# Attention on one core: scores for 1024 queries at a time with 512 moving columns, weight sums per query pair, and the first V loads held

## The chip, the cores and the metric

The kernel runs on one core of a Trainium2 chip. The metric is the device time of the whole program in microseconds (us). PE is TensorE, PEld its weight loads, DVE is VectorE, ACT ScalarE, POOL GpSimd, SP SyncE.

## The reference

```python
# q, k, v: (8, 2048, 512) float32
scores = np.matmul(q, k.transpose(0, 2, 1)) / np.sqrt(512)
attn_weights = special.softmax(scores, axis=-1)
return np.matmul(attn_weights, v)
```

## The kernel before

Both matrix products are done as blocks of two by two with seven products in place of eight: the operands' sums are made on DVE, the products' sums on ACT and DVE, or in the bank (the stretch of accumulator memory) that the matmuls add up in. A batch is 4 blocks of 512 queries (one block is a "quarter" below). While PE multiplies the weights of block g with V (the PV products), it also scores block g+1 (the QK products), in 28 "slots" that alternate the two kinds. Only the first block's scores are done plainly, with eight products, since nothing has been summed yet.

The QK product of a group (cut): two pairs of key blocks, 256 queries each, so four matmuls of 256 columns.

```python
for j in range(G):              # G = 2 pairs of key blocks, QH = 256 queries
    for c in range(2):
        nc.tensor.matmul(
            dst[:, j * QH:(j + 1) * QH], lhs[:, j, c, :], rhs[:, :, c, :],
            start=(n in (1, 5) and j == 0 and c == 0), stop=(c == 1), ...)
```

The weight sums for PV are made for a whole group as soon as its last exponential is there, for all 256 columns (cut):

```python
def p_sums(g, n):
    js = slice(n * G, (n + 1) * G)
    a11, a21 = left[0][:, js], right[:, js, 0]
    a12, a22 = left[1][:, js], right[:, js, 1]
    return [lambda: add(s1[:, js], a21, a22), lambda: sub(s2[:, js], s1[:, js], a11),
            lambda: sub(a21, a11, a21), lambda: sub(s4[:, js], a12, s2[:, js])]
```

At the start Q's and K's first chunks are transposed on PE, later ones by DMA. The first four V loads are issued ahead of the loads of Q's third and fourth chunks (cut):

```python
load("k", 0, 1, (2, 2)); load("k", 0, 2); load("k", 0, 3, ...); load("q", 0, 1, ...)
for c in range(NCH):
    load_v(0, c)
load("q", 0, 2, ...); load("q", 0, 3, ...)      # these two are transposed by DMA
```

The softmax here doesn't subtract the row's maximum and nothing guards it: scores larger than these inputs give would overflow.

Of the kernel before, what the change touches and what calls it, by code (L numbers as in the profile page):

```python
# [12 lines left out]
def kernel(  # L13
# [26 lines left out]
    EXP = mybir.ActivationFunctionType.Exp  # L40
    MULT = mybir.AluOpType.mult
# [4 lines left out]
    QTW = 512  # L46
    NQS = QTW // P
    NQT = T // QTW
# [4 lines left out]
    QH = QTW // 2  # L53
    VP = D + 8
    TP = H + 8
    inv_sqrt_d = float(1.0 / np.sqrt(D))

    G = 2
    NG = NJ // G
    COPY = mybir.ActivationFunctionType.Copy  # L60

    const = ctx.enter_context(tc.tile_pool(name="const", bufs=1))
    stage = ctx.enter_context(tc.tile_pool(name="stage", bufs=4))
    kpool = ctx.enter_context(tc.tile_pool(name="kpool", bufs=5))
    qpool = ctx.enter_context(tc.tile_pool(name="qpool", bufs=3))
    vpool = ctx.enter_context(tc.tile_pool(name="vpool", bufs=2))
    ppool = ctx.enter_context(tc.tile_pool(name="ppool", bufs=2))
    opool = ctx.enter_context(tc.tile_pool(name="opool", bufs=4))
# [18 lines left out]
    qT, kT = {}, {}  # L87
    staged = {}
    vs = {}
# [33 lines left out]
    def operands(what):  # L123
        pool = kpool if what == "k" else qpool
        raw = pool.tile([P, CH, ND, P], F16, tag=what + "raw")
        sums = [pool.tile([P, 2, 2, P], F16, tag=what + f"s{n}", name=what + f"s{n}") for n in (1, 2, 4)]
        return [raw] + sums

    def dma_transpose(what, b, c):
        src = staged.pop((what, b, c))  # L130
        t = operands(what)
        nc.sync.dma_start_transpose(
            out=t[0][:].rearrange("p n c r -> p (n c) r"),
            in_=src[:].rearrange("p n d -> p (n d)"),
        )
        (kT if what == "k" else qT)[b, c] = t

    def transposed(what, b, c, n, src, w, copy):
        if n == 0:
            (kT if what == "k" else qT)[b, c] = operands(what)  # L140
        t = (kT if what == "k" else qT)[b, c]
        tr = psum["px"].tile([P, 2, ND, P], F16, tag="px", name="tr")
        for m in range(w):
            for dc in range(ND):
                nc.tensor.transpose(  # L145
                    tr[:, m, dc, :], src[:, n + m, dc * P:(dc + 1) * P], ident[:]
                )
        copy(out=t[0][:, n:n + w], in_=tr[:, 0:w])

    def pe_transpose(what, b, c, n0=0, n1=CH):  # L150
        src = staged[what, b, c]
        for n in range(n0, n1, 2):
            transposed(what, b, c, n, src, 2, nc.scalar.copy if n else nc.vector.tensor_copy)
        if n1 == CH:
            staged.pop((what, b, c))

    def first_transpose(what, n):
        transposed(what, 0, 0, n, staged[what, 0, 0], 1, nc.vector.tensor_copy)

    def k_blocks(t):  # L160
        w = t[0][:].rearrange("p (j s) c r -> p j s c r", s=2)
        return w[:, :, 0, 0:2], w[:, :, 0, 2:4], w[:, :, 1, 0:2], w[:, :, 1, 2:4]

    def q_blocks(t):
        w = t[0]
        return w[:, 0:2, 0:2], w[:, 2:4, 0:2], w[:, 0:2, 2:4], w[:, 2:4, 2:4]
# [3 lines left out]
    def k_sums(b, c):  # L170
        t = kT[b, c]
        a11, a12, a21, a22 = k_blocks(t)
        _, s1, s2, s4 = t
# [7 lines left out]
    def q_sums(b, c):  # L181
        t = qT[b, c]
        b11, b12, b21, b22 = q_blocks(t)
        _, t1, t2, t4 = t
        return [
            lambda: sub(t1[:], b12, b11),
            lambda: sub(b12, b22, b12),  # L187
            lambda: sub(t2[:], b22, t1[:]),
            lambda: sub(t4[:], b21, t2[:]),
        ]  # L190

    def new_v(b):
        vh = vpool.tile([P, NJ, 2, VP], F16, tag="vh")
        t1 = vpool.tile([P, NJ, TP], F16, tag="t1")
        t2 = vpool.tile([P, NJ, H], F16, tag="t2")
        t4 = vpool.tile([P, NJ, H], F16, tag="t4")
        nc.gpsimd.memset(vh[:, :, 1, D:D + 1], 1.0)
        nc.gpsimd.memset(t1[:, :, H:H + 1], 1.0)
        vs[b] = (vh, t1, t2, t4)

    def load_v(b, c):
        dst = vs[b][0][:].rearrange("p j s d -> p (j s) d")
# [3 lines left out]
    def v_sums(b, c):  # L206
        vh, t1, t2, t4 = vs[b]
# [4 lines left out]
            lambda: sub(t1[:, js, 0:H], b12, b11),  # L212
            lambda: sub(b12, b22, b12),
            lambda: sub(t2[:, js], b22, t1[:, js, 0:H]),
            lambda: sub(t4[:, js], b21, t2[:, js]),  # L215
        ]

    def new_p(g):
        left = [ppool.tile([P, NJ, QH], F16, tag=f"left{s}", name=f"left{s}") for s in range(2)]
        right = ppool.tile([P, NJ, 2, QH], F16, tag="right")  # L220
        sums = [ppool.tile([P, NJ, QH], F16, tag=f"s{n}", name=f"s{n}") for n in (1, 2, 4)]
        pts[g] = (left, right, sums)
# [4 lines left out]
    def plain_tile(g, kb):  # L227

        b, qt = divmod(g, NQT)
        if kb == 0:  # L230
            new_p(g)
        st = bank("qz" if kb % 3 == 2 else "qx")
        c, n = divmod(kb, CH)
        for dc in range(ND):
            nc.tensor.matmul(  # L235
                st[:], kT[b, c][0][:, n, dc, :], qT[b, qt][0][:, :, dc, :],
                start=(dc == 0), stop=(dc == ND - 1),
            )
        left, right, _ = pts[g]
        exp(left[kb % 2][:, kb // 2, :], st[:, 0:QH])  # L240
        exp(right[:, kb // 2, kb % 2, :], st[:, QH:QTW])

    def plain_half(g, j, half):

        b, qt = divmod(g, NQT)
        if j == 0 and half == 0:
            new_p(g)
        st = bank("qx")
        kt, qt_ = kT[b, j // G][0], qT[b, qt][0]
        for s in range(2):  # L250
            for dc in range(ND):
                nc.tensor.matmul(
                    st[:, s * QH:(s + 1) * QH], kt[:, 2 * (j % G) + s, dc, :],
                    qt_[:, 2 * half:2 * half + 2, dc, :],
                    start=(s == 0 and dc == 0), stop=(dc == ND - 1), skip_group_check=True,
                )
        left, right, _ = pts[g]
        if half:
            exp(right[:, j], st[:].rearrange("p (s q) -> p s q", s=2))
        else:  # L260
            for s in range(2):
                exp(left[s][:, j, :], st[:, s * QH:(s + 1) * QH])

    class Group:


        def __init__(self, g, n):
            self.g, self.n = g, n
            self.js = slice(n * G, (n + 1) * G)
            b, qt = divmod(g, NQT)  # L270
            self.a, self.b = kT[b, n], qT[b, qt]

        def product(self, n):
            a11, a12, a21, a22 = k_blocks(self.a)
            b11, b12, b21, b22 = q_blocks(self.b)
            _, s1, s2, s4 = self.a
            _, t1, t2, t4 = self.b
            if n == 1:
                if self.n == 0:
                    new_p(self.g)  # L280
                self.left, self.right, _ = pts[self.g]
# [13 lines left out]
            for j in range(G):  # L295
                for c in range(2):
                    nc.tensor.matmul(  # L297
                        dst[:, j * QH:(j + 1) * QH], lhs[:, j, c, :], rhs[:, :, c, :],
                        start=(n in (1, 5) and j == 0 and c == 0), stop=(c == 1),
                        skip_group_check=True,  # L300
                    )
            getattr(self, f"after{n}", lambda: None)()

        def two(self, t):
            return t[:].rearrange("p (j q) -> p j q", j=G)

# [5 lines left out]
        def after5(self):  # L312
            self.cz = czpool.tile([P, G, 2, QH], F32, tag="cz")
            nc.scalar.copy(out=self.cz[:, :, 1, :], in_=self.two(self.z))  # L314

        def after6(self):
            nc.scalar.copy(out=self.cz[:, :, 0, :], in_=self.two(self.x))  # L317

        def after7(self):
            nc.vector.tensor_add(self.cz[:, :, 1, :], self.two(self.x), self.cz[:, :, 1, :])  # L320

        def after3(self):
            nc.vector.tensor_add(self.cz[:, :, 0, :], self.two(self.z), self.cz[:, :, 0, :])  # L323

        def after4(self):
            exp(self.left[1][:, self.js, :], self.two(self.x))

        def after2(self):
            exp(self.left[0][:, self.js, :], self.two(self.y))

        def exp_right(self):
            exp(self.right[:, self.js], self.cz[:])

    def p_sums(g, n):
        left, right, (s1, s2, s4) = pts[g]
        js = slice(n * G, (n + 1) * G)
        a11, a21 = left[0][:, js], right[:, js, 0]
        a12, a22 = left[1][:, js], right[:, js, 1]
# [6 lines left out]

    class Pair:
# [3 lines left out]
        def __init__(self, g, i):  # L350
            self.g, self.i, self.done = g, i, 0

        def product(self, n):
            g, i = self.g, self.i
            left, right, (s1, s2, s4) = pts[g]
            vh, t1, t2, t4 = vs[g // NQT]
            cols = slice(i * P, (i + 1) * P)
            self.apart = g == NP - 1 and i == 1
            own = "q" if self.apart else "p"
# [4 lines left out]
            elif n == 5:  # L364
# [4 lines left out]
                3: (lambda j: s4[:, j, cols], lambda j: vh[:, j, 1, H:D + 1], "z"),  # L369
                4: (lambda j: right[:, j, 1, cols], lambda j: t4[:, j, :], "x"),  # L370
                5: (lambda j: s1[:, j, cols], lambda j: t1[:, j, 0:H + 1], "z"),
                6: (lambda j: s2[:, j, cols], lambda j: t2[:, j, :], "x"),
# [22 lines left out]
        def store(self, o, half, ds=slice(0, D)):  # L395
            b, qt = divmod(self.g, NQT)
# [273 lines left out]
```

## Time and profile before

| | before |
|---|---|
| device time, median of 3 | 807.06 us |
| span of the profiled run | 805.1 us |
| PE busy, weight loads busy | 99%, 88% |
| DVE busy, ACT busy | 73%, 71% |
| matmuls | 7244 |

The lines themselves stand in the prediction. The reading that counts for PE is from start to start: what one matmul adds to the time.

### The profile page before, as it was taken

The numbers are of one execution on the slowest core, as the hardware profiler recorded it, in microseconds if no ns is written. First come the engines' busy times: TensorE is split into PE (matmuls) and PEld (weight loads), VectorE is DVE, ScalarE is ACT, GpSimd is POOL, SyncE is SP. The second block draws the span as 40 slices with busy tenths as digits, with TensorE's granted clock in tenths as the row PEclk, the third lists the DMA queues.
The fourth block names the chain that finished last, engine by engine and source line by source line (L and its number), as shares of the span: only waits on it lengthen the run. The fifth ranks groups of instructions, "written<-read, shape, count | busy, mean of one in ns | idle before, by whom it ended". The sixth has DMA issues, their size and how long they took to land.

```text
span 805.1 us, 18445 instructions
## 1 busy us (share of the span) xinstructions
PE 798.2 (99%) x7244; PEld 705.1 (88%) x7244; DVE 591.4 (73%) x1477; ACT 571.1 (71%) x1039; POOL 72.7 (9%) x117
## 2 busy tenths in 40 slices
PE   8999999999999999999999999999999999999998
PEld 5788888888888888888888888888888888888887
DVE  4977787787767778677777777777777777766653
ACT  5767767767767777677677677677777776776773
POOL 4020103000030000300002000110002001000000
PEclk9999999999999999999999999999999999999999
DMA  9999966989379992998829997299972998921112
GB/s 207 202 182 179 166 129 116 209 151 183 92 125 216 153 173 70 155 219 142 154 79 162 208 152 154 64 183 197 172 142 67 189 198 158 156 69 46 54 40 79
DMA packets 190246, 116.56 MB, mean 145 GB/s; under 512 B 124496, under 2 KB 172880, under 8 KB 190160
## 3 DMA queue, kind: packets, MB, share of 16 engines
q0 software_dynamic: 49648, 49.29, 39.5%
q1 hardware_dynamic: 140368, 66.08, 39.3%
q8 instruction: 56, 0.92, 0.5%
q14 instruction: 30, 0.25, 0.1%
q10 hardware_dynamic: 144, 0.03, 0.0%
HBM read 100.70 MB, written 33.55 MB: 167 GB/s over the span
## 4 chain that ended last, share of the span: by engine, by line
PE 96%; DVE 2%; DMA 2%; POOL 0%; ACT 0%; issue 0%; SPq 0%; DVEq 0%
PE t L380 48%; PE t L297 46%; DMA stage<-in_k_dram 1%; PE t L235 1%; DMA first<-in_q_dram 1%; PE tr L145 0%; POOL stage L107 0%; DVE t L215 0%; DVE o L391 0%; DVE cz L323 0%; DVE right L342 0%; DVE s L340 0%; ACT o L388 0%; DVE raw L187 0%; DVE s L341 0%
## 5 line engine op out<-in xcount | busy, mean ns | idle before, releaser
L297 PEld LDWEIGHTS <-raw 128*128 128x128 f16 x1984 | 194.1, 98 | 23.4 <-issue 0.6
L388 ACT ACTIVATE o<-t,r 128x256 f32<-128x256 f32 x256 | 122.5, 478 | 128.6 <-DVE r L408 105.7
L297 PE MATMUL t<-raw 128*128 128x256 f16 x1488 | 203.0, 273 | 0.0
L225 ACT ACTIVATE left<-t 128x512 f16<-128x512 f32 (+1 forms) x264 | 156.8, 595 | 21.4 <-PE t L297 18.9
L380 PEld LDWEIGHTS <-s 128*128 128x128 f16 x1536 | 150.3, 98 | 18.5 <-issue 0.2
L297 PEld LDWEIGHTS <-ks 128*128 128x128 f16 x1488 | 145.6, 98 | 17.9 <-issue 0.8
L391 DVE SCALAR_TENSOR_TENSOR o<-t,r,o 128x256 f32<-128x256 f32 x192 | 92.4, 482 | 81.3 <-PE t L380 48.3
L297 PE MATMUL t<-qs,ks 128*128 128x256 f16 x992 | 139.0, 273 | 0.5 <-ACT t L310 0.4
L225 ACT ACTIVATE right<-cz 128x1024 f16<-128x1024 f32 x124 | 132.7, 1070 | 1.5 <-DVE cz L320 1.5
L380 PE MATMUL t<-t,s 128*128 128x257 f16 (+1 forms) x1024 | 133.1, 273 | 0.0
L380 PE MATMUL t<-vh,left 128*128 128x256 f16 x1024 | 132.7, 273 | 0.0
L314 ACT COPY cz<-t 128x512 f32<-128x512 f32 x124 | 72.8, 587 | 67.3 <-PE t L297 67.3
L380 PEld LDWEIGHTS <-right 128*128 128x128 f16 x1024 | 100.2, 98 | 12.2 <-issue 0.6
L320 DVE TENSOR_TENSOR cz<-t,cz 128x512 f32<-128x512 f32 x124 | 85.2, 687 | 34.6 <-PE t L297 34.6
L380 PEld LDWEIGHTS <-left 128*128 128x128 f16 x1024 | 100.2, 98 | 11.6
L323 DVE TENSOR_TENSOR cz<-t,cz 128x512 f32<-128x512 f32 x124 | 84.8, 684 | 1.9 <-PE t L297 1.9
L297 PE MATMUL t<-qs,raw 128*128 128x256 f16 x496 | 74.4, 273 | 0.5 <-DVE cz L320 0.5
L297 PE MATMUL t<-raw,ks 128*128 128x256 f16 x496 | 74.4, 273 | 0.0
L340 DVE TENSOR_TENSOR s<-right 128x512 f16<-128x512 f16 x128 | 54.0, 422 | 27.2 <-ACT right L225 22.2
L317 ACT COPY cz<-t 128x512 f32<-128x512 f32 x124 | 73.2, 591 | 0.2 <-PE t L297 0.2
L310 ACT COPY t<-t 128x512 f32<-128x512 f32 x124 | 70.7, 570 | 3.3 <-ACT o L388 0.3
L380 PE MATMUL t<-vh,s 128*128 128x257 f16 x512 | 66.7, 273 | 0.0
(51 smaller groups left out, 614.1 us busy)
## 6 DMA issues: line engine op xcount, KB each, us to landing
out_dram<-o SPq DMA_DIRECT2D x127, 256.0 KB, 2.8
vh<-in_v_dram POOLq DMA_DIRECT2D x32, 512.0 KB, 14.9
stage<-in_k_dram POOLq DMA_DIRECT2D x29, 512.0 KB, 8.5
stage<-in_q_dram POOLq DMA_DIRECT2D x28, 512.0 KB, 10.3
vh<-in_q_dram POOLq DMA_DIRECT2D x3, 512.0 KB, 20.3
raw<-stage SPq DMA_TRANSPOSE x56, 6.5
first<-in_q_dram SPq DMA_DIRECT2D x2, 256.0 KB, 3.6
first<-in_k_dram SPq DMA_DIRECT2D x2, 256.0 KB, 3.8
```

The source lines that it names most:

```text
L225: nc.scalar.activation(out=out_, in_=in_, func=EXP, scale=inv_sqrt_d)
L235: nc.tensor.matmul(st[:], kT[b, c][0][:, n, dc, :], qT[b, qt][0][:, :, dc, :], start=(dc == 0), stop=(dc == ND - 1),)
L297: nc.tensor.matmul(dst[:, j * QH:(j + 1) * QH], lhs[:, j, c, :], rhs[:, :, c, :], start=(n in (1, 5) and j == 0 and c == 0), stop=(c == 1) ...
L310: nc.scalar.copy(out=self.y[:], in_=self.x[:])
L314: nc.scalar.copy(out=self.cz[:, :, 1, :], in_=self.two(self.z))
L317: nc.scalar.copy(out=self.cz[:, :, 0, :], in_=self.two(self.x))
L320: nc.vector.tensor_add(self.cz[:, :, 1, :], self.two(self.x), self.cz[:, :, 1, :])
L323: nc.vector.tensor_add(self.cz[:, :, 0, :], self.two(self.z), self.cz[:, :, 0, :])
L340: lambda: add(s1[:, js], a21, a22),
L380: nc.tensor.matmul(dst[:, 0:width], lhs(j), rhs(j), start=(first and j == 0), stop=(j == NJ - 1), skip_group_check=True,)
L388: nc.scalar.activation(out=out_, in_=src, func=COPY, scale=r[:])
L391: nc.vector.scalar_tensor_tensor(out=out_, in0=src, scalar=r[:], in1=out_, op0=MULT, op1=ADD)
```

## The change

The intent is fewer, longer instructions for the same arithmetic. 1024 queries are scored together, so that a product of one pair of key blocks has 512 moving columns (columns of the operand that streams past the loaded weights). PV is unchanged in shape. To make room, weight sums are held for one pair of query blocks (128 columns each) at a time instead of for the whole block, K's operands and V's sums are single-buffered, and V's sums fall into one quarter. The plainly scored first part is now 1024 queries. The core of the diff, with cuts:

```diff
-    QTW = 512
+    QH = 512
+    QW = 2 * QH
...
-            for j in range(G):
-                for c in range(2):
-                    nc.tensor.matmul(
-                        dst[:, j * QH:(j + 1) * QH], lhs[:, j, c, :], rhs[:, :, c, :],
...
+            for dc in range(2):
+                nc.tensor.matmul(
+                    dst[:], lhs[:, j, dc, :], rhs[:, :, dc, :],
+                    start=(n in (1, 5) and dc == 0), stop=(dc == 1),
...
+    def p_sums(g, which, j0=0, j1=NJ):
...
+                spool.tile([P, NJ, P], F16, tag=f"s{n}", name=f"s{n}") for n in (1, 2, 4)
...
+    FIRST = "a1 a5 b1 a3 a2 a6 a7 b5 a4 b3 b2 b6".split()
...
+        return {2 * n + (5 if g == 0 else 1): x for n, x in enumerate(order)}
...
+    VSUMS = (0, 1, 2, 3, 5, 6, 8, 10, 12, 14, 15, 16, 17, 18, 19, 20)
...
+    dma_transpose("q", 0, 2)
+    dma_transpose("q", 0, 3)
+
+    nc.gpsimd.tensor_copy(out=gate[:], in_=qraw[1][:, 2 * NT - 1, ND - 1, 0:1])
+    for c in range(NCH):
+        load_v(0, c)
```

The copy into `gate` reads the last element that the second of the two transposes writes. The V loads stand behind it in GpSimd's program: in the trace the copy waits 18.67 us for that transpose, which lands at 31.90, and the first V load is issued at 32.48. This is "the hold".

## The prediction

> **What bounds the kernel now.** I read the page's busy line first, then the chain of waits, then the tensor engine's timeline, because only start-to-start distances tell a busy tensor engine from one at its peak.
>
> ```profile
> PE 798.2 (99%) x7244; PEld 705.1 (88%) x7244; DVE 591.4 (73%) x1477; ACT 571.1 (71%) x1039; POOL 72.7 (9%) x117
> ...
> PE 96%; DVE 2%; DMA 2%; POOL 0%; ACT 0%; issue 0%; SPq 0%; DVEq 0%
> ```
>
> PE is busy 99% of the span and carries 96% of the chain that ended last; VectorE and ScalarE have a quarter of the span free. Now the PE timeline in mid-kernel (start, length, line, operation, shapes, count):
>
> ```profile
> 303.36 0.60 PE L297 MATMUL t<-raw 128*128 128x256 f16 x4
> 303.79 0.60 PE L297 MATMUL t<-qs,ks 128*128 128x256 f16 x4
> 304.23 1.04 PE L380 MATMUL t<-vh,s 128*128 128x257 f16 x8
> 305.11 0.60 PE L297 MATMUL t<-qs,ks 128*128 128x256 f16 x4
> 305.55 0.60 PE L297 MATMUL t<-qs,raw 128*128 128x256 f16 x4
> 305.98 0.27 PE L380 MATMUL t<-vh,left 128*128 128x256 f16 x1
> ```
>
> Take start to start, not the printed lengths, which overlap. 303.36 to 305.98 holds 24 matmuls: 2.62/24 = 109.2 ns each, with no gap. L297 is the scores (QK), L380 weights times V (PV). And the same view at the start, where the kernel already has matmuls of 512 columns:
>
> ```profile
> 16.48 1.07 PE L145 MATMUL tr<-ident,stage 128*128 128x128 f16 x16 [0.33 <-DMA stage<-in_k_dram]
> 17.38 3.62 PE L235 MATMUL t<-raw 128*128 128x512 f16 x16
> 20.84 1.06 PE L145 MATMUL tr<-ident,vh 128*128 128x128 f16 x16
> ...
> 27.80 0.60 PE L297 MATMUL t<-raw 128*128 128x256 f16 x4
> ```
>
> Sixteen of 512 columns take 20.84 - 17.38 = 3.46 us, 216.2 ns each. Two of 256 take 218.4. The seven-product stream starts at 27.80. Last, the PE waits after 30 us, and windows of one quarter of a batch each:
>
> ```profile
> PE t L297 <- DVE cz L320: 0.5, 1, 0.5
> ```
>
> ```profile
> 297.00:321.50 24.50, 24.50 (x227) 21.96 (x225) 19.93 (x50) 17.73 (x33) 0.00 (x0) 1.00 0.39 99
> 321.50:346.00 24.50, 24.50 (x227) 21.91 (x225) 17.09 (x42) 17.73 (x33) 6.10 (x10) 1.00 0.94 153
> ```
>
> The columns are length, PE, PEld, DVE, ACT, POOL busy, granted clock, DMA share, GB/s. PE never idles in them even where DVE is at 19.9 of 24.5. One listed wait of 0.5 us in 775: there is no wait here for a change to remove.
>
> **What the Trainium skill says.** (1) "TensorE: Matmul & The Clock Gate", section "Wait — 56ns, not 53.3ns?": a warm matmul starts N/2.4 GHz plus about 2.5 ns after the one before. That gives 109.2 ns at 256 and 215.8 at 512; the trace agrees (109.2, 216.2). So halving the instruction count at equal columns saves about 2.5 ns per pair and no more. (2) The same page, "Back-to-back issue gap", has about 131 ns for each N=512 matmul in a stream with weight loads. The trace shows 216.2 in just such a stream, so I do not use it; on it, one would hope for 140 us. (3) "Perfetto Trace Analysis", section "Identifying the Most-Contended Engine", prefers LDWEIGHTS busy to matmul busy as the measure of headroom. It is 88% here, and the change cuts it; but the distance between matmuls is that of columns alone, so fewer weight loads should buy nothing. (4) "VectorE: DVE Perf Modes", section "Side-by-side: where the cycles go for N=2048 bf16": some 150 cycles fixed, plus half a cycle per element for a two-tensor 16-bit op. For 512 elements 414 cycles, 431 ns; the trace has 417 to 425. For 1024 I estimate 0.69 us (0.42 + 256 cycles at 0.96 GHz).
>
> **The change part by part.**
>
> Scores, main stream. Before: 31 blocks of 512 queries x 4 groups x 7 products x 4 matmuls = 3472, of 256 columns: 3472 x 109.2 = 379.1 us. After: 15 spans of 1024 queries x 8 groups x 7 x 2 = 1680, of 512 columns: 1680 x 215.9 = 362.7. That is **-16.4 us**, but 12.1 of it is that one block of 512 queries leaves the stream; the instruction saving alone is 4.3.
>
> Scores of the first span, in plain form. Before 12 key blocks x 4 matmuls of 512 columns, and 32 of 256. After, 28 tiles x 4 of 512 and the same 32 of 256: 64 more at 216 ns = **+13.8 us**. The 12.1 us of seven products come back as 13.8 of eight, on the path, as PE alone sets the end. The sum of PE work is **-2.6 us**.
>
> PV: 32 x 2 x 7 x 8 = 3584 matmuls before and after, same shapes. Nothing.
>
> Weight sums: 128 x 4 ops of 512 elements become 64 x 4 of 1024 (some split): 512 x 0.42 = 215 us against 256 x 0.69 = 177. Q's sums fall likewise. DVE has about 40 us less work, all beside PE: worth nothing directly, but it pays for denser places. V's 16 sums now fall into one quarter of a batch instead of two. Counted from start to start (some 0.05 us below the printed lengths, as neighbours overlap) that quarter has: 8 cz additions 5.0, 6 final additions 2.6, 4 reciprocals 0.5, pair sums 5.1 plus 0.5 for the split, V sums 5.9, one of Q 0.6: some 20 of 24.3 us. That is the 19.9 at which no PE gap shows above. ScalarE's work per group is unchanged, 17.7 of 24.5.
>
> Start. The plain part runs after the same first 9.3 us of loads. The first Q and K chunks land when they did; the second Q chunk takes the landing slot of K's third chunk (16.43), just in time for its transposes at 16.5; K's third and fourth slip to about 19.5 and 22, and are wanted after some 23 us and 31 us. So the stream starts at 27.80 + 13.8 = 41.6. Q's other two chunks land near 24.5 and 27 (2.5 us apart, as the V loads before: 24.38, 26.90, 29.41 in the list of DMA issues), their transposes at 4.5 us more, near 31.6. Only then V's loads are issued: the first about 6 us later (a lone 512 KB load took 5.7 to 6.7), the others 2.5 apart: 38, 40.5, 43, 45.5. The first PV product stands at slot 5 of the stream, near 43.8, its last two key blocks want the fourth load: PE waits **about 1 us** there. DVE, which is strictly in order, stands at V's sums meanwhile and then has about 18 us of work in 19: I give that **0.7 us**.
>
> End. Without scores now run two quarters instead of one: 112 more PV products with nothing between. Before, the last 128 took 786.76 to 801.5, 14.7 us for 14.0: 0.7 lost. I add **0.5 us** for the second, and **0.5 us** in all for the dense batch starts and single-buffered K, whose transposes have at least 14 slots of 0.87 us to land, for a median of 6.5.
>
> Against this about 1.5 us of small gaps near 27.8 to 48 go and are re-made; I count half of it gone: -0.8. Sum: -2.6 + 1.0 + 0.7 + 0.5 + 0.5 - 0.8 = **-0.7 us**, rounded toward the careful tuning that the held V loads betray: -1.3. Predicted **805.8 us**.
>
> **The rivals.** (a) Pure PE arithmetic: all new waits are hidden. For it: DVE and ACT slack, and no PE waits before. Then -2.6 to -4, 803 to 804.5. (b) The start becomes DMA-bound: the V loads, held behind two transposes, come several us late. For it: DMA is at nine tenths in the first slices, and a transpose that shared it took 10 us against 4.5. Against: after the two Q chunks nothing else is queued. It costs 3 to 5 us once: 808 to 811. (c) Single-buffered K and V sums, and the crowded DVE, stall every batch. Against: each overwrite stands behind its last reader by one slot or more. At 1 us per batch, 7 us: 812; for slower by 2% it would need over 2 us per batch, 16 in all. (d) 512-column matmuls or half as many weight loads free PE far more, as the 131 ns or the 88% would suggest. Against: 216 ns measured. Then tens of us, below 780.
>
> **Range and chances.** (a) and my sum together carry most; (b) is the likeliest miss, (c) the tail. Range 802.8 to 811. Two per cent is 16 us: faster needs (d), 0.01; slower needs (c) at its worst, 0.03; within, 0.96.
>
> **What would show it.** Right: L297's main group of about 1680 matmuls at 216 ns start to start; PEld busy well down (by some 170 us) with no gain from it; the stream's first product near 41.6; V's last load landing near 45 with a PE wait of 1 us; DVE busy some 40 us less. Wrong: main-stream distances other than 216; PE gaps repeated every 98 us by a DVE or DMA releaser; a start later than 43; or a wait of several us in the last 25.

## The result, and the profile after

The changed kernel took 806.44 us (median of 4, 805.94 to 807.17) against 806.98 for the kernel before (median of 4). The ratio is 0.9993, with a 95% interval of 0.9976 to 1.0011: no difference is shown. A ratio here is the mean time of one kernel's fast runs over that of the other's of the same rounds, so it is not quite the ratio of the medians.

The page's busy line and chain of the changed kernel:

```profile
PE 796.4 (99%) x5516; PEld 536.1 (67%) x5516; DVE 548.5 (68%) x1213; ACT 570.8 (71%) x1021; POOL 71.4 (9%) x104
...
PE 91%; DMA 6%; SPq 1%; POOL 1%; DVE 0%; issue 0%; ACT 0%; ACTq 0%; POOLq 0%
```

1728 matmuls and as many weight loads are gone. Weight-load time fell by 169 us and DVE by 43 us, yet the span is the same, 805.4 against 805.1 us. New is the 6% of DMA in the chain, where 2% stood.

The PE timeline in mid-kernel (start, length, engine, line, operation, shapes, count); L278 is now QK, L373 PV:

```profile
303.37 1.04 PE L373 MATMUL t<-vt,right 128*128 128x256 f16 x8
304.24 0.59 PE L278 MATMUL t<-qraw,kraw 128*128 128x512 f16 x2
304.67 0.59 PE L278 MATMUL t<-qs,ks 128*128 128x512 f16 x2
305.10 1.04 PE L373 MATMUL t<-vh,s 128*128 128x257 f16 x8
```

A pair of 512 columns takes 0.43 us, where four of 256 took 0.43 to 0.44. Over all 1680 score matmuls the median distance from start to start is 216 ns. The windows of two quarters, with the columns as before (length, PE, PEld, DVE, ACT, POOL, clock, DMA share, GB/s):

```profile
297.00:321.50 24.50, 24.50 (x172) 16.58 (x170) 15.86 (x34) 18.13 (x33) 2.23 (x3) 1.00 1.05 183
321.50:346.00 24.50, 24.50 (x172) 16.59 (x171) 18.75 (x44) 17.87 (x33) 0.74 (x1) 1.00 0.36 85
```

PE has no idle time here, as before. Now the start, where the stream of seven-product scores begins:

```profile
41.65 0.59 PE L278 MATMUL t<-qraw,kraw 128*128 128x512 f16 x2
42.08 0.59 PE L278 MATMUL t<-qs,ks 128*128 128x512 f16 x2
42.99 0.59 PE L278 MATMUL t<-qs,ks 128*128 128x512 f16 x2 [0.31 <-DVE vt L208]
43.50 0.59 PE L278 MATMUL t<-qraw,ks 128*128 128x512 f16 x2
43.93 0.82 PE L373 MATMUL t<-vh,left 128*128 128x256 f16 x6
46.29 0.38 PE L373 MATMUL t<-vh,left 128*128 128x256 f16 x2 [1.54 <-DMA vh<-in_v_dram]
```

Six of the eight matmuls of the first PV product run; the last two wait 1.54 us, until the fourth V load has landed at 46.25. The longest of PE's waits in the list of waits from 41 us on:

```profile
PE t L373 <- DMA vh<-in_v_dram: 1.5, 1, 1.5
PE t L373 <- ACT o L381: 0.9, 1, 0.9
PE t L278 <- DVE vt L208: 0.3, 1, 0.3
```

**Where the gain went.** I added up the start-to-start distances of PE by line, in both traces, up to the last matmul's start:

| us | before | after | difference |
|---|---|---|---|
| start of the score stream | 27.80 | 41.65 | +13.85 |
| score matmuls of the stream (3472, 1680) | 381.24 | 364.44 | -16.80 |
| PV matmuls (3583 distances each) | 392.32 | 395.27 | +2.95 |
| last matmul starts at | 801.36 | 801.36 | 0.00 |

The sum closes. Of the 2.95, 1.7 is the V wait with its restart, 1.0 comes where V's sums are dense (0.2 in the first batch, 0.1 in each of the seven later ones), and 0.2 more is lost at the end. The wait for ACT near 419 us, 1.0, lies in the row of the score matmuls, as each distance is counted to the matmul that begins it. That row also had 1.9 us of small gaps up to 48 us before, and has 0.6 after. Without gaps a distance is 109.17 ns before and 215.82 after, which makes -16.5 for the row.

### The profile page after: what moved, and what is told of

The parts are those of the page before. It is cut to its first block, busy times and chain, and to the rows that moved or that the text cites. A ratio compares the mean times of both kernels' runs of the same rounds, so it can differ in the third digit from the quotient of the medians.

```text
span 805.4 us, 14513 instructions
## 1 busy us (share of the span) xinstructions
PE 796.4 (99%) x5516; PEld 536.1 (67%) x5516; DVE 548.5 (68%) x1213; ACT 570.8 (71%) x1021; POOL 71.4 (9%) x104
## 4 chain that ended last, share of the span: by engine, by line
PE 91%; DMA 6%; SPq 1%; POOL 1%; DVE 0%; issue 0%; ACT 0%; ACTq 0%; POOLq 0%
PE t L373 48%; PE t L278 43%; DMA vh<-in_q_dram 2%; DMA vh<-in_v_dram 1%; DMA out_dram<-o 1%; SPq L143 1%; DMA cz<-in_q_dram 1%; DMA qraw<-vh 1%; SPq L128 0%; POOL vh L200 0%; POOL vh L118 0%; ACT o L381 0%; SPq L391 0%; POOL stage L118 0%; DVE stage L132 0%
## 5 line engine op out<-in xcount | busy, mean ns | idle before, releaser
L278 PE MATMUL t<-qraw,kraw 128*128 128x512 f16 x720 | 194.7, 379 | 0.0
L373 PEld LDWEIGHTS <-s 128*128 128x128 f16 x1536 | 150.2, 98 | 58.1 <-issue 1.1
L278 PEld LDWEIGHTS <-kraw 128*128 128x128 f16 x960 | 93.9, 98 | 62.3
L373 PE MATMUL t<-vh,left 128*128 128x256 f16 x1024 | 132.9, 273 | 1.5 <-DMA vh<-in_v_dram 1.5
L373 PE MATMUL t<-vt,s 128*128 128x257 f16 (+1 forms) x1024 | 133.0, 273 | 0.9 <-ACT o L381 0.9
L278 PE MATMUL t<-qs,ks 128*128 128x512 f16 x480 | 133.1, 379 | 0.3 <-DVE vt L208 0.3
L220 ACT ACTIVATE right<-cz 128x1024 f16<-128x1024 f32 x120 | 127.3, 1061 | 1.1 <-DVE cz L298 1.1
L373 PEld LDWEIGHTS <-left 128*128 128x128 f16 x1024 | 100.2, 98 | 38.9 <-issue 1.7
L373 PEld LDWEIGHTS <-right 128*128 128x128 f16 x1024 | 100.1, 98 | 38.5 <-issue 0.4
L292 ACT COPY cz<-t 128x512 f32<-128x512 f32 x120 | 70.2, 585 | 72.6 <-PE t L278 72.2
L278 PEld LDWEIGHTS <-ks 128*128 128x128 f16 x720 | 70.4, 98 | 47.5 <-issue 0.8
L278 PE MATMUL t<-qraw,ks 128*128 128x512 f16 x240 | 71.4, 379 | 0.0
L278 PE MATMUL t<-qs,kraw 128*128 128x512 f16 x240 | 71.4, 379 | 0.0
L295 ACT COPY cz<-t 128x512 f32<-128x512 f32 x120 | 69.8, 582 | 0.2 <-PE t L278 0.2
L373 PE MATMUL t<-vt,right 128*128 128x256 f16 x512 | 67.2, 272 | 0.0
L373 PE MATMUL t<-vh,s 128*128 128x257 f16 x512 | 66.7, 273 | 0.0
```

Source lines behind the costliest of these rows:

```text
L220: nc.scalar.activation(out=out_, in_=in_, func=EXP, scale=inv_sqrt_d)
L278: nc.tensor.matmul(dst[:], lhs[:, j, dc, :], rhs[:, :, dc, :], start=(n in (1, 5) and dc == 0), stop=(dc == 1), skip_group_check=True,)
L292: nc.scalar.copy(out=self.cz[:, 1, :], in_=self.z[:])
L295: nc.scalar.copy(out=self.cz[:, 0, :], in_=self.x[:])
L373: nc.tensor.matmul(dst[:, 0:width], lhs(j), rhs(j), start=(first and j == 0), stop=(j == NJ - 1), skip_group_check=True,)
```

## The experiments

Ten kernels ran, in three calls. Each was timed in five rounds beside the kernel before. "Less" and "more" are against the changed kernel unless said otherwise.

**The changed kernel again** (no edit).

> The changed kernel once more, as the base for the others of this call. Theory A (PE columns set the time; the small gain is eaten at the start): 806.4 us as before, within 0.5; the wait of about 1.5 us for the fourth V load at 44.5 us comes again, since it follows from the order of the loads; the single gap of about 1 us near 418 us, behind a late output store, may come elsewhere or not at all. Rival B (that gap is part of the change's cost): it comes at 418 us again.

It took 807.27 us (804.41 to 808.04), ratio 0.9993 again. The V wait came again, 1.15 us of idle PE. So did a wait for ACT, now at 420 us, with 0.6 us of PE time lost in place of 1.0. In the first trace ACT waited 2.24 us there for an output store. Two stores issued at 408.7 and 409.3 took 10 us each, beside a transpose that was 18 us under way and two Q loads. Both traces of the changed kernel itself show such a loss near that place, and of the nine variants only one (0.4 us). So this loss comes and goes. Its cause stays open; the run cannot decide for A or B on this point.

The stream of this run began 1.7 us later. PE's transposes of Q's second chunk and the start of the stream, first in the changed kernel's trace above:

```profile
16.52 1.06 PE L153 MATMUL tr<-ident,vh 128*128 128x128 f16 x16
...
41.65 0.59 PE L278 MATMUL t<-qraw,kraw 128*128 128x512 f16 x2
```

and in this run's:

```profile
18.22 1.07 PE L153 MATMUL tr<-ident,vh 128*128 128x128 f16 x16
...
43.36 0.59 PE L278 MATMUL t<-qraw,kraw 128*128 128x512 f16 x2
```

The chunk landed at 16.35 and at 18.17. In the eight traces with the whole plain part and the hold, the stream begins 25.1 us after these transposes, and they wait for the chunk in all but one. It lands between 14.96 and 18.17, so the stream begins between 41.06 and 43.36. A start in one trace is thus known to no better than 1 us or so.

**Only the instruction size undone.**

```diff
             for dc in range(2):
-                nc.tensor.matmul(dst[:], lhs[:, j, dc, :], rhs[:, :, dc, :], ...)
+                for hf in range(2):
+                    nc.tensor.matmul(
+                        dst[:, hf * 256:(hf + 1) * 256], lhs[:, j, dc, :],
+                        rhs[:, hf * NT // 2:(hf + 1) * NT // 2, dc, :], ...)
```

> Every score matmul of 512 columns in the main stream is issued as two of 256 with the same weights; all else is as in the changed kernel. Theory A: only the fixed 2.4 to 2.5 ns per instruction comes back, 1680 x 2.4 = 4.0 to 4.3 us, so 810.5 us. Rival C (weight loads matter, so halving them was worth more than the distance between matmuls says): 1680 more weight loads of 98 ns cost well over 5 us. Rival D (the number of instructions is worth nothing): 806.4.

It took 811.36 us, 4.1 more than the repeat of the changed kernel (ratio 1.0055, 1.0043 to 1.0067). Its timeline:

```profile
300.56 1.04 PE L279 MATMUL t<-qraw,kraw 128*128 128x256 f16 x8
301.44 1.04 PE L375 MATMUL t<-vh,left 128*128 128x256 f16 x8
302.31 1.04 PE L279 MATMUL t<-qs,ks 128*128 128x256 f16 x8
```

Eight matmuls take 0.87 to 0.88 us, 109 ns each. By the sums of distances the score stream takes 3.7 us more than in the repeat, whose sum holds 0.6 us of the wait for ACT; the V wait was 1.1 us longer in this trace. Without gaps two matmuls of 256 take 218.3 ns and one of 512 takes 215.8: 2.5 ns per pair, 4.2 us for 1680. Weight loads were back at 700.2 us busy (86%), 164 us more than in the repeat. So A stands: the gain of 512 columns is some 4 us, a fixed part of 2.5 ns for each pair of matmul and weight load that goes. Which of the two it belongs to, the run cannot tell. C and D fall.

**No hold.** The copy into `gate` ahead of the V loads is left out.

> The first V loads no longer wait for Q's last transpose; they queue straight behind Q's loads and would land about 30 to 37 us. Theory A: the wait of 1.5 us for V at 44.5 us goes, all transposes still land before 42, 804.8 us. Rival E (the hold is needed): the two transposes[...] take 10 to 18 us each in place of 4.7, and Q's sums and with them the stream's first products come late; then the same or slower, 806 to 812.

It took 817.36 us, ratio 1.0127 (1.0114 to 1.0140). PE's longest waits in the list of waits:

```profile
PE t L278 <- DVE qs L191: 8.7, 1, 8.7
PE t L278 <- DMA qraw<-vh: 1.7, 1, 1.7
```

The two Q transposes from issue to landing, in the window from 20 to 28 us, without the hold:

```profile
DMA to landing us min/median/max: 18.8/21.7/24.7
```

and the same view of the changed kernel:

```profile
DMA to landing us min/median/max: 4.6/4.8/4.9
```

V's four loads, the next two Q loads and a K load, issued between 12.0 and 24.9 us, are now under way beside them; by what means they hold the transposes up is not shown. The second transpose lands at 51.19 us, where it was 31.90. DVE cannot make Q's sums before, and PE stands still. And the stall costs more than its length. The windows around it (same columns; the clock is third from the end):

```profile
42.00:51.50 9.50, 0.60 (x2) 0.11 (x2) 0.21 (x1) 0.57 (x1) 0.13 (x1) 0.70 1.24 184
51.50:55.80 4.30, 3.76 (x12) 1.72 (x13) 4.13 (x9) 1.17 (x2) 1.48 (x2) 0.50 0.85 141
```

After 8.7 us of idling PE works on at half clock for over 4 us (matmuls of 512 columns start 427 ns apart), some 2 us lost. Here my theory A was wrong: it took the hold for dispensable. Rival E holds, and its upper figure of 812 was still too low.

**Less plain work**: for the second half of the queries and the last eight key blocks, one of four matmuls is issued (cut; the stop flag goes with it). Its output is wrong, which doesn't matter for the time.

```diff
-        for dc in range(ND):
+        last = 0 if half and kb >= 8 else ND - 1
+        for dc in range(last + 1):
```

> Wrong on purpose: eight of the plain tiles of the first span do one of their four matmuls, so 24 matmuls of 512 columns, 5.2 us of PE work, fall away just before the stream. Theory A (PE sets the start, up to the 1.7 us that V is late): at most nothing is gained, because the fourth V load lands at 46.3 us whatever PE does: the stream starts at 36.5, the wait for V grows from 1.7 to about 6 us or spreads over the slots before it, 806 us. Rival F (the plain scores' extra 1.7 us sit on the path and are what ate the gain): 801.2 us.

It took 807.68 us, ratio 1.0009 (0.9995 to 1.0023): 5.2 us of PE work less, and nothing gained. The same PV product in its timeline:

```profile
38.96 0.38 PE L374 MATMUL t<-vh,left 128*128 128x256 f16 x2
40.36 0.38 PE L374 MATMUL t<-vh,left 128*128 128x256 f16 x2 [1.02 <-DMA vh<-in_v_dram]
42.92 0.42 PE L374 MATMUL t<-vh,left 128*128 128x256 f16 x2 [2.18 <-DMA vh<-in_v_dram]
45.45 0.58 PE L374 MATMUL t<-vh,left 128*128 128x256 f16 x2 [2.11 <-DMA vh<-in_v_dram]
```

PE takes each V chunk as it lands (the four landed at 36.79, 40.32, 42.88 and 45.41) and finishes the product at the last. The matmuls after it ran at half clock to 49.7 (granted clock 0.50 from 45.0 on), by their distances 2.2 us lost; that blurs the comparison, but without it the gain would still be 0.8 us by the traces' last matmuls, the 0.8 us by which V landed earlier in this run (the store wait of the changed kernel's trace taken off as well). So A: the first PV product ends when V has landed, even with 5.2 us less for PE to do before. F falls for this kernel.

**Hold on one transpose.** The copy reads the last element of the first Q transpose instead of the second.

```diff
-    nc.gpsimd.tensor_copy(out=gate[:], in_=qraw[1][:, 2 * NT - 1, ND - 1, 0:1])
+    nc.gpsimd.tensor_copy(out=gate[:], in_=qraw[1][:, NT - 1, ND - 1, 0:1])
```

> The first V loads wait for the first of the two Q chunks' transposes, not for both, so they are issued some 2.3 us earlier, while the second transpose is still under way. Theory A (the start is bound by the landing of the fourth V load, and the transposes suffer only from V loads that overlap them for long): the fourth V load lands near 44 us, the wait before the PV product goes, the second transpose lands 1 to 4 us later than 31.9 and still before it is wanted at 40; 1.5 to 2 us less than the changed kernel, 804.7 us. Rival E2 (any overlap with V is ruinous): the second transpose takes 15 us or more, as it did with no hold at all, and the time is 810 us or more.

It took 804.30 us, ratio 0.9967 (0.9954 to 0.9979). V landed at 36.27, 39.06, 41.66 and 44.17, and the second transpose, under way for 2.6 us when the first V load was issued, landed at 31.77 after 4.3 us: no slower at all. The product that had been split by the wait:

```profile
43.94 1.04 PE L373 MATMUL t<-vh,left 128*128 128x256 f16 x8
44.81 1.03 PE L278 MATMUL t<-qraw,kraw 128*128 128x512 f16 x4
```

runs through. The stream begins at 41.65 as in the changed kernel's trace, so the two compare well: the last matmul starts 2.8 us earlier, 1.7 of it the V wait and 1.1 the wait behind the output store, which did not come. The intervals of the times only just touch. A stands, E2 falls: here an overlap of 1.7 us with V's loads cost nothing, where loads over the whole stretch made the two transposes 14 and 20 us longer.

**DVE's work given back.** Each weight sum runs as two of half the key pairs (cut).

```diff
-        js = slice(j0, j1)
+        jm = (j0 + j1) // 2
+        for js in (slice(j0, jm), slice(jm, j1)):   # in each of the four steps
```

> Each of the weight-sum operations of a query pair is issued as two of half the size, so VectorE gets the instructions and the busy time back that the change took from it (some 30 us). Theory A (VectorE lies beside PE): 806.7 us, within 1 of the changed kernel, no new PE wait over 0.3 us except where V's sums are dense. Rival G (VectorE is near the path, and the lighter sums are what pays for the change): 2 us or more slower.

It took 808.44 us, ratio 1.0008 (0.9995 to 1.0021); the changed kernel's 0.9993 lies just below this interval, and its own (0.9976 to 1.0011) overlaps it. DVE was busy 568.1 us, 20 more, and not the 30 expected. By the distances PE loses 0.24 us in each batch where V's sums are dense, in place of 0.10, about 1.0 us more over all batches; this trace's V wait was also 0.4 us longer. That is the crowding A allowed for, and not G's 2 us. By the distances this half of the saved DVE time is worth about 1 us; the times alone do not exclude somewhat more.

**PV later.** The first quarter's PV products start at slot 9 (`9 if g == 0`) in place of 5; the hold stays as in the changed kernel.

> The first group's PV products start at slot 9 in place of 5; the hold stays. Theory A: score products fill the time until the fourth V load lands, the wait of 1.3 to 1.7 us shrinks below 0.5; but four more slots of bare scores are dense for ScalarE, which gives up to 1 us back: 805.5 us. Rival H (the PV order is on the path, later PV pushes everything): 807 us or more.

It took 804.26 us, ratio 0.9970 (0.9958 to 0.9983). In its timeline:

```profile
45.07 1.04 PE L373 MATMUL t<-vh,left 128*128 128x256 f16 x8
45.94 0.59 PE L278 MATMUL t<-qs,ks 128*128 128x512 f16 x2
46.81 0.59 PE L278 MATMUL t<-qs,kraw 128*128 128x512 f16 x2 [0.27 <-DVE cz L298]
```

The product runs through and 0.4 us comes back as a wait for DVE. V's fourth load landed at 45.10 and so still after 43.3, where slot 5 begins in this run. It is thus the wait, and not an earlier V, that went; 0.6 us of this trace's gain is a stream that began earlier, as Q's second chunk landed at 14.96. H falls.

**Hold on one transpose, and V's sums one slot earlier.**

```diff
-    VSUMS = (0, 1, 2, 3, 5, 6, 8, 10, 12, 14, 15, 16, 17, 18, 19, 20)
+    VSUMS = (0, 1, 2, 3, 5, 6, 8, 10, 12, 13, 14, 15, 16, 17, 18, 19)
```

> The hold on the first Q chunk as in the run of that alone, and V's sums one slot earlier from the tenth on. Theory A: besides the 1.5 to 2 us of the hold, the wait of 0.1 us in each of the eight batches goes, 0.7 us in all: 804 us. If the sums move other waits onto PE, the same as the hold alone or worse.

It took 803.87 us, ratio 0.9958 (0.9944 to 0.9971). By the distances the loss of 0.1 us is gone in the seven later batches; the first batch has a list of its own and keeps it. The difference to the hold alone is within the intervals, so it is seen in the traces but not in the times.

**All three**: that kernel, and PV from slot 9.

> The hold on the first Q chunk alone, V's sums one slot earlier, and the first group's PV products from slot 9. Theory A: nothing waits for V, and the eight waits of 0.1 us are gone; since the hold and the later PV cure the same wait, they do not add: 803 to 804 us, no more than 0.5 below the run without the later PV.

It took 803.78 us, ratio 0.9955 (0.9942 to 0.9969). As expected the later PV adds nothing once the hold is shorter. It beats the kernel before by 0.45%, and the changed kernel, by the two ratios, by 0.4%; these intervals do not overlap.

**All three, with eight plain matmuls less** (three of four matmuls in eight plain tiles). Its output is wrong, which doesn't matter for the time.

> Wrong on purpose: the kernel of the three changes, with one of four matmuls left out in eight plain tiles of the first span, 8 x 216 ns = 1.7 us of PE work, the price of scoring 512 more queries with eight products in place of seven. Theory A: with V out of the way PE work at the start is on the path again, so 1.7 us less than the kernel with the three changes, where 5.2 us less had bought nothing in the changed kernel. If the start is still bound by transfers: no gain.

It took 802.53 us, ratio 0.9940 (0.9927 to 0.9954), 1.2 us less than the kernel of the three changes. The intervals overlap, so the times alone show little. The start of the stream with all plain matmuls (the kernel of the three changes):

```profile
41.96 0.59 PE L278 MATMUL t<-qraw,kraw 128*128 128x512 f16 x2
```

and with eight less:

```profile
40.47 0.59 PE L279 MATMUL t<-qraw,kraw 128*128 128x512 f16 x2
```

That is 1.49 us earlier, though Q's second chunk landed 0.24 later here. Counted from PE's transposes of that chunk, the plain part lasts 23.41 us in place of 25.14: 1.73 less, the eight matmuls. The last matmul starts 1.6 us earlier (0.4 us of it is a store wait that only the other trace has; 0.3 is lost here to a wait for DVE, and 0.24 to the chunk). With V out of the way PE work at the start counts again.

## Why the prediction was right

**The sum.** The terms of the prediction, and what the two profiled runs show by distances:

| us | predicted | shown |
|---|---|---|
| score stream, without gaps | -16.4 | -16.5 |
| plain first part | +13.8 | +13.85 |
| V wait | +1.0 | +1.7 |
| DVE after it | +0.7 | +0.2 |
| end | +0.5 | +0.25 |
| dense batches, single-buffered K | +0.5 | +0.7 |
| small gaps at the start | -0.8 | -1.4 |
| wait behind an output store | none | +1.1 |
| sum | -0.7 | -0.1 |

Unrounded, what is shown adds up to 0.0: the last matmul starts at 801.36 us in both traces. The two large terms came from the distances and were right. That the small ones add up so near is in part luck, as their errors cancel.

**The bound.** Right. PE sets the time before and after, but for the waits named here, and the fixed part of 2.5 ns per pair is all that the longer matmuls save. The split run measured it alone: 4.1 us by the medians, 4.2 by the distances without gaps, for the 4.3 predicted.

**The plain block.** Right in length; that the stream begins at 41.65, predicted 41.6, is luck to some part. The prediction had Q's second chunk land at 16.43, just in time; it landed at 16.35 in this trace, but at 18.17 in the repeat, where the stream began at 43.36, past the 43 that the prediction gave as a sign of being wrong. PE work is not all that sets this start. The role of the plain work was also subtler than the sum said. In the changed kernel those 1.7 us are hidden behind V, as the run with less plain work shows; they are a cost only once V is early, as the last run shows. The prediction added the plain work and the V wait as if they were independent. Their sum was right, though removing the plain work would only have grown the wait.

**The V wait.** Right in mechanism, undersized. Predicted landings of 38, 40.5, 43 and 45.5; measured 38.15, 40.77, 43.73 and 46.25. The first load took the estimated time, the next three 2.5 to 3.0 us each. The wait was 1.54 us and 1.7 with its restart, where the sum had 1.0.

**DVE.** The 0.7 us for DVE after V's late landing was oversized: after the landing, two waits of 0.1 us are all that the first quarter shows. (The 0.31 us at 42.99 comes before it. It is put down to DVE in this trace and to ACT's copy in the last run's, and the kernel before has one like it, 0.36 us, at 29.20.) The estimate of 0.69 us for a weight sum of 1024 elements was measured at 0.68 to 0.69. The 40 us less of DVE work were 43. The 0.5 us for the dense batches was 0.73 (seven of about 0.1); these gaps, one in each batch, are in small the sign that was to show rival (c). The single-buffered K shows in no PE wait.

**End.** The extra quarter without scores lost 0.47 us between 774 and 781, for 0.5 predicted. But the last quarter lost 0.36 where the end before had lost 0.58, so the net is 0.25. The prediction's 0.7 us for the old end was misread: a QK product of four matmuls (788.50 to 788.94) lies in that stretch, and 0.3 is left without it.

**What was missed.** The intermittent wait behind a late output store, 1.0 us in the profiled run, was not foreseen. The time came out 0.6 us above the predicted 805.8, and 1.5 above in the repeat; both are within the range, and 0.6 us is within what runs of one kernel differ by (805.94 to 807.17 here). The last 0.6 us of the prediction were rounded off for careful tuning, with no term behind them.

**The rivals.** Rival (d) is refuted: weight-load time fell by 169 us without effect. Rival (a), all waits hidden, comes nearly true with the shorter hold: 804.30 us, and 803.87 with V's sums a slot earlier, inside its 803 to 804.5. Rival (b) is partly what happened: the start did become bound by transfers, by 1.7 us in place of 3 to 5. What the prediction did not see is the other side of (b). It gave 10 us for a transpose beside other loads; without the hold the two took 18.8 and 24.7. The hold is worth some 10 us in this schedule, and it costs under 2 us as placed.

## What to carry to other kernels

Where matmuls follow each other without a gap, count columns: doubling the length of an instruction saved only about 2.5 ns per pair here, and halving the weight loads nothing beyond that. When the steady state cannot give more, look at the fill: follow each first load to its first use, and remember that work removed there may only lengthen the wait for the slowest load. A hold that protects one transfer from another should end as early as the protected transfer allows, here one transpose sooner.

## What the Trainium skill lacked or had wrong

- "TensorE: Matmul & The Clock Gate", section "Back-to-back issue gap": about 131 ns per matmul of N=512 in a stream with weight loads. The 1680 here start 216 ns apart (median), in a stream where each has its weight load. The page's other formula, N/2.4 plus 2.5 ns, fits.
- "Perfetto Trace Analysis", section "Identifying the Most-Contended Engine": takes weight-load busy time, next to the share of peak arithmetic, as a measure of TensorE's headroom. It is no such measure here: it went from 88% to 67% with the time unchanged, and in the split run to 86% for 4 us.
- "DMA: Bandwidth & Descriptors", section "Rules for kernel authors": says a transpose next to ordinary DMAs needs nothing. That is about correctness, and results were correct here; but beside a queue of 512 KB loads two transposes took 18.8 and 24.7 us to land, in place of 4.9 and 4.6 (the second is queued behind the first). I found no number on the page for a transpose beside loads.
